# Pool bias of four token tiles added by accumulating transfers in a PoolFormer and ConvFFN layer

## The chip, the cores and the metric

The kernel runs on one core of one Trainium2 chip. The metric is the device time of one execution in microseconds. The core has five engines with a queue of instructions each: TensorE (PE, whose weight loads are listed as PEld), VectorE (DVE), ScalarE (ACT), GpSimd (POOL) and SyncE (SP). An engine works its instructions in their order; semaphores let one wait for another. Transfers (DMA) are issued by SP, ACT or POOL and move on 16 DMA engines. A transfer that adds its source to its destination (an accumulating transfer) is issued by POOL here.

## What is computed

One layer (DEPTH is 1) for 1024 tokens of 1024 channels, float32: a causal pooling mixer, then a gated FFN with a causal convolution of width 3.

```python
h = rms_norm(x, norm_mix_g)
# pooling, per group of 256 channels, windows 2, 4, 8, 16:
groups.append(window_sum / count - h_group)
y = pool_scale * (einsum('bsgc,gcd->bsgd', d, pool_w) + pool_b)
x = x + y
h = causal_depthwise_conv(rms_norm(x, norm_ffn_g) @ ffn_w_in, conv_w, conv_b)
val, gate = split(h, 2)
x = x + (silu(gate) * val) @ ffn_w_out
```

The bias that matters here is one row of 1024 numbers, pool_scale * pool_b, that is added to every token.

## The kernel before

**Mixer stage (the first 75 us of the span).** The tokens are eight tiles of 128. For tile j, in this order: `stat` (L442 on) takes the mean square on ACT (`junk_a`, L178) and refines the root on DVE (L180 to L183); `mixer_norm` scales the band matrices by it (`bandr`, L187); `window_sums` multiplies x by them on PE (`psd`, L201), which gives the pooled tile transposed; DVE adds the first 16 tokens' part from the tile before (L270); ACT copies it to SBUF (`dh`, L271); `mixer_out` multiplies by the scaled weights on PE (`psy`, L286), and two more matmuls with a matrix of ones add the bias, which lies in two rows, a high and a low part, so that the sum is exact enough (L289, `bias_hl`); DVE adds x (L292, "the residual add"), in place, which gives x1; SP writes x1 to DRAM. Then the statistics of x1 (`junk_b`, `st_b`), the normed tile `n` (L304), its transposes on PE (`pst`, L319), and the copies and splits that make the FFN's operands from them: ACT copies to `n2f` (L328, L331), ACT and DVE write a high part and a rest (`B`, `T`; L338, L339). The second four tiles are combined with the first four (L350), so they complete `T1`.

All of `psd`, `psy` and `pst` come from one pool of three PSUM tiles, taken in turn (`bank2`): a group of matmuls waits until the tile of three groups before has been read.

**FFN, one level of Strassen's scheme.** A weight tile (`win`, 1 MB, 22 of them) has four parts A11, A12, A21, A22, each 128x512. Products are formed from A11, A12, A22 and from the sums S1 = A21+A22, S2 = A11+S1, S3 = A11+A21, S4 = A12+S2. S3 and S1 of all weight tiles, and S2 and S4 of the first two, are made by accumulating transfers of 256 KB that POOL issues (L361), each waiting for the one it builds on and for the splits that still read its destination; the other sums are made by DVE. Each operand is then split in two (`split`, L91 on ACT, L92 on DVE). For weight tiles 0 and 1, `sums_in(n, 0)` makes S3 and S1, `sums_in(n, 1)` S2 and S4. S2 overwrites A11, so it waits for the A11 split; S4 overwrites A12 and waits for the A12 split.

**Order of the work.** The mixer's last loop, `for j in range(2, NS + 4)`, weaves tile j's steps together: windows of tile j-1, output of tile j-2, transposes of tile j-4. `prep_event(k)` puts a split of a weight tile between them: k = 0 and 1 are A11 of weight tiles 0 and 1, k = 2 and 3 their A12. `tc.issue_after(marks[...])` holds instructions behind a given one in the planned order; the tile framework's scheduler then puts the instructions of each engine in a fixed order.

Of the kernel before, what the change touches and what calls it, by code (L numbers as in the profile page):

```python
# [7 lines left out]
F32 = mybir.dt.float32  # L8
# [3 lines left out]
ALU = mybir.AluOpType  # L12
PSUM = bass.MemoryType.PSUM

P = 128
S = 1024
D = 1024
# [22 lines left out]
NOPS_A = 3  # L40

XBUFS = 5

PAD = 24

# [18 lines left out]
def trunk_kernel(ctx: ExitStack, tc: tile.TileContext, x, consts, par, rows, pool_w, w_in, w_out, out):  # L64
    nc = tc.nc

    const = ctx.enter_context(tc.tile_pool(name="const", bufs=1))
    dram = ctx.enter_context(tc.tile_pool(name="dram", bufs=1, space=bass.MemoryType.DRAM))
# [4 lines left out]
    work = ctx.enter_context(tc.tile_pool(name="work", bufs=1, side="right"))  # L73
# [24 lines left out]
    xs = {}  # L98
# [36 lines left out]
    for g, w in enumerate(WINDOWS):  # L135

        m = band[:, g, :]
# [30 lines left out]
    def rstd_of(src, name, halves=False):  # L168
        junk = pp.tile([P, D], BF16, tag="junk", name=f"junk_{name}")
        st = pp.tile([P, 8], F32, tag="st", name=f"st_{name}", bufs=8)  # L170
        part, first, ms, root, q, inv, half = (st[:, i : i + 1] for i in range(7))
        bias = eps_t
        if halves:
            bias = first
            nc.scalar.activation(junk[:, :NH], src[:, :NH], AF.Square, accum_out=half)
            nc.vector.tensor_scalar(first, half, D * EPS, None, op0=ALU.add)
            src, junk = src[:, NH:], junk[:, NH:]
        nc.scalar.activation(junk, src, AF.Square, accum_out=part)  # L178
        marks[name] = nc.scalar.activation(root, part, AF.Sqrt, bias=bias).ins
        nc.vector.tensor_scalar(ms, part, first if halves else D * EPS, None, op0=ALU.add)  # L180

        nc.vector.scalar_tensor_tensor(q, root, root, ms, op0=ALU.mult, op1=ALU.add)
        nc.vector.reciprocal(inv, q)  # L183
        return root, inv

# [30 lines left out]
    wps = pp.tile([P, 2 * NG, GRP], F32, tag="wps", name="wps")  # L216
# [13 lines left out]


    b8 = rows8[:, 1, :]

    def pool_bias():
        marks["bias"] = nc.scalar.activation(bias8[:, 0, :], b8, AF.Copy).ins
        marks["bias_dve"] = nc.vector.tensor_tensor(bias8[:, 1, :], b8, bias8[:, 0, :].bitcast(F32), ALU.subtract).ins
        for l in range(2):
            m = nc.sync.dma_start(bias_hl[l : l + 1, :].bitcast(F32), bias8[:, l, :].bitcast(F32)).ins
        with tc.issue_after(m):
            for j in range(3, NS):  # L240
                load_x(j)
            nc.sync.dma_start(par_sb[:, :GM], par[:, :GM])
# [14 lines left out]
    def window_sums(j):  # L257
        ps = bank2(f"psd{j}")
        marks[f"psd{j}"] = windows(ps, xs[j], bands.pop(j))
        return ps  # L260

    def mixer_window(j, ps=None):
        ps = window_sums(j) if ps is None else ps
        dh = ds[j] = pp.tile([P, NK, P], F32, tag="dh", name=f"dh{j}", bufs=2)
        ps3 = ps.rearrange("p (c s) -> p c s", c=NK)
        first = ps3[:, :, :HALO]
        if j == 0:
            marks["first"] = nc.vector.tensor_tensor(first, first, fac, ALU.mult).ins
        elif j > 1:
            nc.vector.tensor_tensor(first, first, edges[:, :, j * HALO : (j + 1) * HALO], ALU.add)  # L270
        marks[f"dh{j}"] = nc.scalar.activation(dh, ps3, AF.Copy).ins  # L271
# [9 lines left out]
    def mixer_out(j, stats=True):  # L281
        dh = ds.pop(j)
        ps = bank2(f"psy{j}")
        for c in range(NK):
            o = ps[:, c // 2 * GRP : (c // 2 + 1) * GRP]
            nc.tensor.matmul(o, dh[:, c, :], wps[:, c, :], start=c % 4 == 0, stop=False, skip_group_check=True)  # L286
        for h in range(2):
            cols = slice(h * NH, (h + 1) * NH)
            m = nc.tensor.matmul(ps[:, cols], ones, bias_hl[:, cols], start=False, stop=True, skip_group_check=True)  # L289
        marks[f"psy{j}"] = m.ins  # L290
        x1 = n2s[j] = xs.pop(j)
        marks[j] = nc.vector.tensor_tensor(x1, ps, x1, ALU.add).ins  # L292
        nc.sync.dma_start(x1_dram[j * P : (j + 1) * P, :], x1)
        if stats:
            mixer_out_stats(j)
# [62 lines left out]
    def sums_in(n, step):  # L358

        def more(out, a):  # L360
            nc.gpsimd.dma_start(out, a, accum_op=ALU.add)  # L361

        a11, a12, a21, a22 = (raws[n][:, i, k * NH : (k + 1) * NH] for i in range(2) for k in range(2))
        if step == 0:
            s3 = sums[n, "S3"] = tmp(f"S3_{n}")
            nc.sync.dma_start(s3, w_in[order[n]][:, 0, :NH])
            more(s3, a21)
            more(a21, a22)
        else:
            sums[n, "S2"] = a11  # L370
            more(a11, a21)
            sums[n, "S4"] = a12
            more(a12, a11)
# [95 lines left out]
    def prep_event(k):  # L469
        if k < len(events):  # L470
            n, p = events[k]
            prep_in(n, STEPS[p][0])
# [49 lines left out]
        mixer_edges()  # L522
    with tc.issue_after(marks["edges_pe"]):
        sums3 = window_sums(3)
    with tc.issue_after(marks["dh1+"]), tc.issue_after(marks["edges"]):
        mixer_out_stats(0)
    for j in range(2, NS + 4):
        if 3 < j < NS:
            with tc.issue_after(marks[1]) if j == 4 else nullcontext():
                mixer_norm(j)  # L530
        if 1 <= j - 1 < NS and j > 2:
            mixer_window(j - 1, {3: sums2, 4: sums3}.get(j))
        if j == NS + 1:
            with tc.issue_after(marks[f"n{NS - 2}"]):
                prep_event(4)
                prep_event(6)
        if 1 <= j - 2 < NS:
            with tc.issue_after(marks["S4", 0] if j == NS + 1 else marks[f"band{min(j, 4)}"]) if j > 2 else nullcontext(), tc.issue_after(marks["psd3"]):
                mixer_out(j - 2)
        if 0 <= j - 2 < NS:  # L540
            with tc.issue_after(marks["dh1+"]):
                ffn_norm(j - 2)
        if 0 <= j - 4 < NS:
            ffn_operand(j - 4)
        if j in (4, 6):
            load_in(j // 2 - 2)
            sums_in(j // 2 - 2, 0)
        if 5 <= j <= 8:
            with tc.issue_after(marks[j - 2]), tc.issue_after(marks[f"b{j - 3}"]):
                prep_event(j - 5)  # L550
        if j in (7, 8):
            sums_in(j - 7, 1)
        if j in (8, 10, 11):
            event((8, 10, 11).index(j))
        with tc.issue_after(marks["edges"]):
            stat(j + 1)
            stat(j + 2)
# [156 lines left out]
    for k in range(-SLOOK, len(oevents)):  # L714
        p, f = oevents[k + SLOOK] if k + SLOOK < len(oevents) else (None, 0)
# [8 lines left out]
        with tc.issue_after(lasts[-1]) if lasts else nullcontext():  # L724
# [12 lines left out]
            p, f = oevents[k]  # L737
# [10 lines left out]
        if f == 0 and opens:  # L748
            for i in range(4):
                tag = ("XXYY" if set_ == "X" else "YZZZ")[i]  # L750
# [106 lines left out]
```

## Time and profile before

| what | value |
|---|---|
| time, median of 3 runs | 672.28 us (670.89 to 673.64) |
| profiled execution, its time | 670.79 us |
| profiled execution, its span | 669.0 us |
| PE, DVE, ACT, POOL busy | 663.6, 569.1, 338.8, 47.8 us |
| granted PE clock | 1.00 |
| mixer stage, tile 0's windows to the first product with T1 | 7.6 to 74.9 us |

The profile is of one execution. A row of the timeline has the start in us from the start of the span, the length, the engine, the line of the kernel, the operation, what it writes and reads, and how many were merged; in brackets stands the idle time of the engine before it and what ended that. The buffers' numbers are left out there, so that `x` is any token tile and `win` any weight tile. Of a merged group of matmuls the length reaches from the start of the first to the end of the last, and consecutive groups overlap by the depth of the pipeline; from start to start is what a group costs. A row of the chain of waits has start, length, engine and line only. A DMA queue's row has its packets, MB, and the time of its packets as a share of 16 engines over the window asked for (q0 is the queue of the transfers that POOL issues, q1 that of SP). An issue row gives the KB of each and the median time from issue to landing.

### The profile page before, as it was taken

Reading aid. Unit: us, or ns where it says so; the run is one execution under the profiler, and the core shown is the slowest. Engines: PE = TensorE matmul, PEld = TensorE weight load, DVE = VectorE, ACT = ScalarE, POOL = GpSimd, SP = SyncE. Lnnn points to the kernel's source line nnn. Section 1 sums busy time; section 2 is a strip of 40 time slices with the busy share of each in tenths; the row PEclk is TensorE's granted clock in tenths of the full one; section 3 lists DMA queues with packets and bytes.
Section 4 is the critical chain, followed back from the end, with each engine's and each line's share of the span. In section 5 each row is a group of like instructions: output and inputs, shape, how many; then the busy total and the mean of one; then the engine's idle time right before and its main releaser. Section 6 shows DMA issues by size and latency. Waiting matters only on the chain.

```text
span 669.0 us, 8720 instructions
## 1 busy us (share of the span) xinstructions
PE 663.6 (99%) x3164; PEld 579.2 (87%) x3164; DVE 569.1 (85%) x841; ACT 338.8 (51%) x517; POOL 47.8 (7%) x73
## 2 busy tenths in 40 slices
PE   9999999999999999999999999999999999999997
PEld 7999878888888888888888888888888888888886
DVE  4798999998888888888888888887987988999995
ACT  6696656554544544444544454454554444444441
POOL 3021020111001111111011101100000000000000
PEclk9999999999999999999999999999999999999999
DMA  8983253544444454544444444429999710232231
GB/s 269 326 207 105 85 141 126 167 145 124 133 134 105 123 142 141 143 130 128 135 141 130 113 136 132 111 92 350 332 335 352 269 58 0 62 96 82 62 125 64
DMA packets 41603, 101.23 MB, mean 151 GB/s; under 512 B 4668, under 2 KB 6616, under 8 KB 38744
## 3 DMA queue, kind: packets, MB, share of 16 engines
q1 hardware_dynamic: 34464, 87.55, 37.3%
q0 software_dynamic: 6944, 12.59, 11.3%
q10 hardware_dynamic: 152, 0.53, 0.3%
q8 instruction: 25, 0.41, 0.2%
q14 instruction: 18, 0.15, 0.1%
HBM read 68.14 MB, written 19.92 MB: 132 GB/s over the span
## 4 chain that ended last, share of the span: by engine, by line
PE 96%; DVE 2%; ACT 1%; issue 0%; POOL 0%; ACTq 0%; POOLq 0%
PE oP L771 29%; PE Y L402 25%; PE X L402 17%; PE Z L402 16%; PE psy L286 4%; PE psd L201 2%; PE pst L319 1%; DVE T L339 1%; PE psy L289 1%; PE ps_scale L222 0%; PE idle_ps L149 0%; DVE n2f L580 0%; ACT B L338 0%; PE ps_edges L201 0%; PE ps_gain L248 0%
## 5 line engine op out<-in xcount | busy, mean ns | idle before, releaser
L771 PE MATMUL oP<-oBP,oAP 128*128 128x512 f32 (+1 forms) x924 | 198.9, 378 | 0.1
L771 PEld LDWEIGHTS oP<-oBP,oAP 128*128 128x128 f32 x924 | 174.0, 189 | 25.0 <-DVE oBP L92 0.5
L402 PE MATMUL X<-B,A11s 128*128 128x512 f32 x264 | 61.5, 380 | 0.0
L402 PE MATMUL Y<-T,S3s 128*128 128x512 f32 x264 | 60.8, 380 | 0.4 <-DVE q L431 0.4
L402 PE MATMUL Y<-T,A22s 128*128 128x512 f32 x264 | 60.8, 380 | 0.0
L402 PE MATMUL Z<-T,S1s 128*128 128x512 f32 x264 | 60.8, 379 | 0.0
L402 PE MATMUL X<-B,A12s 128*128 128x512 f32 x264 | 60.6, 379 | 0.0
L402 PE MATMUL Y<-T,S2s 128*128 128x512 f32 x264 | 60.6, 379 | 0.0
L402 PE MATMUL Z<-B,S4s 128*128 128x512 f32 x264 | 60.5, 379 | 0.0
L402 PEld LDWEIGHTS Y<-T,S3s 128*128 128x128 f32 x264 | 49.7, 189 | 8.2 <-DVE q L431 1.2
L402 PEld LDWEIGHTS Y<-T,A22s 128*128 128x128 f32 x264 | 49.7, 189 | 7.9 <-DVE hb L439 0.6
L402 PEld LDWEIGHTS Z<-T,S1s 128*128 128x128 f32 x264 | 49.8, 189 | 7.5 <-DVE T L339 0.4
L402 PEld LDWEIGHTS Z<-B,S4s 128*128 128x128 f32 x264 | 49.8, 189 | 7.3 <-DVE r L436 0.3
L402 PEld LDWEIGHTS Y<-T,S2s 128*128 128x128 f32 x264 | 49.9, 189 | 7.1
L402 PEld LDWEIGHTS X<-B,A11s 128*128 128x128 f32 x264 | 49.7, 189 | 7.3 <-DVE A11s L92 0.4
L402 PEld LDWEIGHTS X<-B,A12s 128*128 128x128 f32 x264 | 49.8, 189 | 7.0
L91 ACT ACTIVATE oBP<-blk 128x512 fp32r<-128x512 f32 x53 | 33.1, 625 | 44.2 <-PE oP L771 30.6
L460 ACT ACTIVATE gate<-gate 128x1024 f32<-128x1024 f32 x22 | 23.2, 1057 | 49.3 <-DVE gate L451 49.3
L91 ACT ACTIVATE oAP<-blk 128x512 fp32r<-128x512 f32 x55 | 34.1, 620 | 19.3 <-DVE blk L350 16.8
L92 DVE TENSOR_TENSOR oBP<-blk,oBP 128x512 fp32r<-128x512 f32 x53 | 36.5, 688 | 8.6 <-ACT oBP L91 6.6
L92 DVE TENSOR_TENSOR oAP<-blk,oAP 128x512 fp32r<-128x512 f32 x55 | 37.7, 685 | 2.6 <-ACT oAP L91 2.6
L450 DVE SCALAR_TENSOR_TENSOR val<-ha,par_sb,val 128x1023 f32<-128x1023 f32 x22 | 28.2, 1283 | 13.2 <-ACT val L449 13.2
(131 smaller groups left out, 958.3 us busy)
## 6 DMA issues: line engine op xcount, KB each, us to landing
win<-in_w_in_dram SPq DMA_DIRECT2D x22, 1024.0 KB, 4.8
g_dram<-val SPq DMA_DIRECT2D x22, 512.0 KB, 2.6
blk<-g_dram SPq DMA_DIRECT2D x33, 256.0 KB, 5.2
blk<-in_w_out_dram SPq DMA_DIRECT2D x31, 256.0 KB, 5.7
win<-win POOLq DMA_DIRECT2D x26, 256.0 KB, 3.5
S<-in_w_in_dram SPq DMA_DIRECT2D x22, 256.0 KB, 3.5
S<-win POOLq DMA_DIRECT2D x22, 256.0 KB, 4.2
A12s<-g_dram SPq DMA_DIRECT2D x22, 256.0 KB, 5.2
```

What stands on the lines that cost most here:

```text
L91: nc.scalar.activation(t[:, 0, :], src, AF.Copy)
L92: m = nc.vector.tensor_tensor(t[:, 1, :], src, t[:, 0, :].bitcast(F32), ALU.subtract)
L201: m = nc.tensor.matmul(ps[:, c * P : (c + 1) * P], src[:, c * P : (c + 1) * P], weights[:, c // 2, :], start=True, stop=True)
L286: nc.tensor.matmul(o, dh[:, c, :], wps[:, c, :], start=c % 4 == 0, stop=False, skip_group_check=True)
L289: m = nc.tensor.matmul(ps[:, cols], ones, bias_hl[:, cols], start=False, stop=True, skip_group_check=True)
L319: nc.tensor.transpose(ps[:, c * P : (c + 1) * P], n2[:, c * P : (c + 1) * P], ident)
L339: return hi, nc.vector.tensor_tensor(l, src, h.bitcast(F32), ALU.subtract).ins
L402: nc.tensor.matmul(bank, a[:, i, ks], woven(b[:, l, k, :]), start=opens and m == 0, stop=m == 11, skip_group_check=not opens)
L450: nc.vector.scalar_tensor_tensor(t[:, 1:], src[:, : S - 1], w[1], t[:, 1:], op0=ALU.mult, op1=ALU.add)
L460: nc.scalar.activation(gate, gate, AF.Silu)
L771: nc.tensor.matmul(bank, a[:, u, i * P : (i + 1) * P], woven(b[:, v, :])[:, c.start // 2 : c.stop // 2, :], start=opens and first, stop=g ...
```

## The change

Three parts.

1. For token tiles 4 to 7 (`BY_DMA = 4`) the two bias matmuls (L289) are left out. In their place the scaled bias row goes from SBUF to DRAM once, comes back spread to 128 rows (`bias_b`, in the buffer that held the edge tokens), and is added to x by an accumulating transfer of 512 KB per tile (`bias_into`), which waits for the tile's windows, since these read x, and which the residual add waits for. All six transfers are issued by POOL.
2. The refinement of the root (L182) is a tensor_scalar with two scalars from SBUF in place of a scalar_tensor_tensor; the result is the same.
3. `prep_event(0)` is issued one loop step later, and `prep_event(2)` moves to the step of `prep_event(1)`; the sum S1 of weight tiles 0 and 1 is issued from a step of its own, behind the bias transfer of tile 4 or 5.

```diff
+BY_DMA = 4
-        nc.vector.scalar_tensor_tensor(q, root, root, ms, op0=ALU.mult, op1=ALU.add)
+        nc.vector.tensor_scalar(q, root, root, ms, op0=ALU.mult, op1=ALU.add)
...
+    bias_row = dram.tile([1, D], F32, tag="bias_row", name="bias_row")
+    biased = {}
+    def bias_spread():
+        biased["tile"] = work.tile([P, D], F32, tag="ha", name="bias_b", bufs=1)
+        nc.gpsimd.dma_start(biased["tile"], bias_row.to_broadcast([P, D]))
+    def bias_into(j):
+        if j >= BY_DMA:
+            biased[j] = nc.gpsimd.dma_start(xs[j], biased["tile"], accum_op=ALU.add).ins
     def pool_bias():
...
+        nc.gpsimd.dma_start(bias_row.rearrange("o (k p) -> (o k) p", p=P), b8)
...
-        for h in range(2):
+        for h in range(0 if j >= BY_DMA else 2):
             cols = slice(h * NH, (h + 1) * NH)
             m = nc.tensor.matmul(ps[:, cols], ones, bias_hl[:, cols], start=False, stop=True, skip_group_check=True)
...
+        if step == 0 and n > 1 or step == 2:
             more(a21, a22)
-        else:
+        if step == 1:
...
     with tc.issue_after(marks["edges_pe"]):
         sums3 = window_sums(3)
+        bias_spread()
...
             mixer_window(j - 1, {3: sums2, 4: sums3}.get(j))
+            bias_into(j - 1)
...
-        if 5 <= j <= 8:
+        if j in (5, 6):
+            with tc.issue_after(biased[j - 1]):
+                sums_in(j - 5, 2)
+        if 6 <= j <= 8:
             with tc.issue_after(marks[j - 2]), tc.issue_after(marks[f"b{j - 3}"]):
-                prep_event(j - 5)
+                for k in {6: (0,), 7: (1, 2), 8: (3,)}[j]:
+                    prep_event(k)
```

What stands where now. In these rows a tile's buffer has its number. Before, token tiles 3 to 7 are x_225, x_227, x_229, x_231 and x_233, and weight tiles 0 and 1 are win_425 and win_550.

POOL, its transfers of the mixer stage, before:

```order
L361 DMA S_0_427<-win_425 128x512
L361 DMA win_425<-win_425 128x512
L361 DMA S_1_552<-win_550 128x512
L361 DMA win_550<-win_550 128x512
L361 DMA win_425<-win_425 128x512
L361 DMA win_550<-win_550 128x512
L361 DMA win_425<-win_425 128x512
L361 DMA win_550<-win_550 128x512
```

And after the change, where token tiles 3 to 7 are x_227, x_229, x_231, x_233 and x_235, and weight tiles 0 and 1 are win_429 and win_551:

```order
L376 DMA S_0_431<-win_429 128x512
L244 DMA x_229<-bias_b 128x1024
L376 DMA win_429<-win_429 128x512
L376 DMA S_1_553<-win_551 128x512
L244 DMA x_231<-bias_b 128x1024
L376 DMA win_551<-win_551 128x512
L376 DMA win_429<-win_429 128x512
L244 DMA x_233<-bias_b 128x1024
L376 DMA win_551<-win_551 128x512
L244 DMA x_235<-bias_b 128x1024
L376 DMA win_429<-win_429 128x512
L376 DMA win_551<-win_551 128x512
```

The three rows of win_425 and of win_429 are S1, S2 and S4 of weight tile 0, in that order, and likewise for tile 1. The bias of tile 7 (x_235) now stands ahead of S4 of weight tile 0. The write of the bias row and its spread come before the first row shown.

DVE, from the residual add of tile 5 to the split of the A12 part of weight tile 0, before:

```order
L292 TENSOR_TENSOR x_229<-psy_573,x_229 128x1024
L92 TENSOR_TENSOR A12s_610<-win_425,A12s_610 128x512
L339 TENSOR_TENSOR B_154<-pst_596,B_154 128x8x64
L180 TENSOR_SCALAR st_b_587<-st_b_587 128x1
L270 TENSOR_TENSOR psd_615<-psd_615,edges 128x8x16
```

After:

```order
L307 TENSOR_TENSOR x_231<-psy_575,x_231 128x1024
L94 TENSOR_TENSOR A11s_610<-win_551,A11s_610 128x512
L354 TENSOR_TENSOR B_155<-pst_596,B_155 128x8x64
L94 TENSOR_TENSOR A12s_613<-win_429,A12s_613 128x512
L182 TENSOR_SCALAR st_b_587<-st_b_587 128x1
L283 TENSOR_TENSOR psd_618<-psd_618,edges 128x8x16
```

The A11 split of weight tile 1 has come behind tile 5's add, and the A12 split of weight tile 0 behind a B part.

ACT, from the copy of tile 4's windows to the copy of tile 5's, before:

```order
L271 ACTIVATE dh_449<-psd_440 128x1024
L91 ACTIVATE A11s_489<-win_425 128x512
L338 ACTIVATE B_154<-pst_475 128x8x64
L178 ACTIVATE junk_b_465,st_b_466<-x_225 128x1024
L179 ACTIVATE st_b_466<-st_b_466,eps_t 128x1
L338 ACTIVATE B_156<-pst_475 128x8x64
L178 ACTIVATE junk_a_492,st_a_493<-x_233 128x1024
L328 ACTIVATE n2f<-pst_475 128x8x2x64
L179 ACTIVATE st_a_493<-st_a_493,eps_t 128x1
L271 ACTIVATE dh_510<-psd_501 128x1024
```

After:

```order
L284 ACTIVATE dh_452<-psd_443 128x1024
L353 ACTIVATE B_155<-pst_479 128x8x64
L180 ACTIVATE junk_b_469,st_b_470<-x_227 128x1024
L353 ACTIVATE B_157<-pst_479 128x8x64
L181 ACTIVATE st_b_470<-st_b_470,eps_t 128x1
L180 ACTIVATE junk_a_494,st_a_495<-x_235 128x1024
L343 ACTIVATE n2f<-pst_479 128x8x2x64
L181 ACTIVATE st_a_495<-st_a_495,eps_t 128x1
L284 ACTIVATE dh_512<-psd_503 128x1024
L93 ACTIVATE A11s_557<-win_429 128x512
```

The split of the A11 part of weight tile 0 has gone from ahead of tile 5's copy to behind it. In both orders ACT later does the S1 and S4 splits of weight tile 0 right before the `n2f` copy of tile 4's transposes.

More of the change, by code (lines that the diff above doesn't have):

```diff
@@ L285, in mixer_out @@
             o = ps[:, c // 2 * GRP : (c // 2 + 1) * GRP]
-            nc.tensor.matmul(o, dh[:, c, :], wps[:, c, :], start=c % 4 == 0, stop=False, skip_group_check=True)
-        for h in range(2):
+            m = nc.tensor.matmul(
+                o, dh[:, c, :], wps[:, c, :], start=c % 4 == 0, stop=j >= BY_DMA and c % 4 == 3, skip_group_check=True
+            )
+        for h in range(0 if j >= BY_DMA else 2):
             cols = slice(h * NH, (h + 1) * NH)
```

## The prediction

> **What bounds the kernel now.** I read the page first: the busy line of TensorE, then what the end of the chain hangs on.
>
> ```profile
> span 669.0 us, 8720 instructions
> PE 663.6 (99%) x3164; PEld 579.2 (87%) x3164; DVE 569.1 (85%) x841; ACT 338.8 (51%) x517; POOL 47.8 (7%) x73
> ```
>
> TensorE works 99% of the span, so a matmul taken away should shorten it, unless its helpers can't go faster. All that the change touches lies in the first 75 us, so next come the busy times of that stretch (columns: window, its length, then PE, weight load, DVE, ACT, POOL busy, clock, DMA share, GB/s).
>
> ```profile
> 20.00:30.00 10.00, 10.00 (x57) 8.93 (x56) 5.80 (x17) 7.27 (x13) 0.00 (x0) 1.00 0.97 339
> 40.00:45.00 5.00, 5.00 (x30) 4.41 (x29) 4.67 (x13) 4.97 (x11) 1.74 (x2) 1.00 0.76 188
> 45.00:50.00 5.00, 5.00 (x31) 4.59 (x30) 4.59 (x10) 4.56 (x8) 0.85 (x1) 1.00 0.88 210
> ```
>
> From 40 to 50 us PE, DVE and ACT are all above 90%: three engines of nearly the same length. The timeline of PE shows the end of tile 4's second half, and tiles 5 to 7:
>
> ```profile
> 42.95 0.81 PE L289 MATMUL psy<-bias_hl,ones 128*128 128x512 f32 x2
> 43.60 1.03 PE L319 MATMUL pst<-cst,n 128*128 128x128 f32 x8
> 44.48 2.05 PE L201 MATMUL psd<-bandr,x 128*128 128x128 f32 x16
> 46.36 3.62 PE L286 MATMUL psy<-wps,dh 128*128 128x256 f32 x16
> 49.63 0.82 PE L289 MATMUL psy<-bias_hl,ones 128*128 128x512 f32 x2
> 52.94 3.62 PE L286 MATMUL psy<-wps,dh 128*128 128x256 f32 x16
> 56.86 1.04 PE L319 MATMUL pst<-cst,n 128*128 128x128 f32 x8
> 64.25 1.91 PE L319 MATMUL pst<-cst,n 128*128 128x128 f32 x16
> ```
>
> Each group starts where the last one ends. Then the chain of waits in order of time: up to 71 us it is PE, then it leaves PE.
>
> ```profile
> 71.58 1.08 PE pst L319 x8
> 72.68 0.61 ACT n2f L331
> 89.27 0.61 DVE q L431
> 89.93 2.21 PE Y L402 x9
> ```
>
> From tile 7's transposes (71.58) to the q2 of the first weight tile (89.27) the end hangs on ACT and DVE, and DVE enters that stretch with tile 7's residual add. So what the change is worth is read from when DVE can start that add, 64.44 in the timeline of DVE:
>
> ```profile
> 38.16 1.22 DVE L292 TENSOR_TENSOR x<-psy,x 128x1024 f32<-128x1024 f32 x1
> 39.29 0.68 DVE L92 TENSOR_TENSOR A11s<-win,A11s 128x512 fp32r<-128x512 f32 x1
> 44.56 1.22 DVE L292 TENSOR_TENSOR x<-psy,x 128x1024 f32<-128x1024 f32 x1
> 47.00 0.15 DVE L180 TENSOR_SCALAR st_b<-st_b 128x1 f32<-128x1 f32 x1
> 48.25 0.21 DVE L182 SCALAR_TENSOR_TENSOR st_b<-st_b 128x1 f32<-128x1 f32 x1
> 50.48 1.22 DVE L292 TENSOR_TENSOR x<-psy,x 128x1024 f32<-128x1024 f32 x1 [0.30 <-PE psy L289]
> 51.62 0.68 DVE L92 TENSOR_TENSOR A12s<-win,A12s 128x512 fp32r<-128x512 f32 x1
> 57.06 1.22 DVE L292 TENSOR_TENSOR x<-psy,x 128x1024 f32<-128x1024 f32 x1 [0.96 <-PE psy L289]
> 63.24 0.68 DVE L92 TENSOR_TENSOR S4s<-win,S4s 128x512 fp32r<-128x512 f32 x1
> 64.44 1.22 DVE L292 TENSOR_TENSOR x<-psy,x 128x1024 f32<-128x1024 f32 x1 [0.53 <-PE psy L289]
> ```
>
> The adds of tiles 5, 6 and 7 wait for PE by 0.30, 0.96 and 0.53 us: PE leads, but DVE is never far behind.
>
> **Removed.** One pair of bias matmuls takes 43.60 - 42.95 = 0.65 us; four pairs are 2.6 us of PE. Were nothing else in the way, the add of tile 7 would come 2.6 us sooner.
>
> **What of it gets through.** Two rows of ACT stand beside tile 4 (the timeline of ACT; the others are used below):
>
> ```profile
> 37.63 0.63 ACT L91 ACTIVATE A11s<-win 128x512 fp32r<-128x512 f32 x1
> 43.40 1.02 ACT L271 ACTIVATE dh<-psd 128x1024 f32<-128x1024 f32 x1
> 56.47 0.64 ACT L91 ACTIVATE S4s<-win 128x512 fp32r<-128x512 f32 x1
> 57.94 0.60 ACT L331 ACTIVATE n2f<-pst 128x512 f32<-128x512 f32 x1 [0.83 <-PE pst L319]
> ```
>
> Tile 6's windows (44.48) take the PSUM that the copy at 43.40 leaves at 44.42: 0.06 us apart. With tile 4's pair gone PE is there at 43.83 and must wait for the copy. The moved A11 split takes 0.6 us of DVE (39.29, up to its successor at 39.89) and its ACT part out of this stretch, and the shorter refinements give some 0.25; walking DVE and ACT through their new order I get the copy at 43.04, 0.36 sooner, and the windows at 44.1. So some 0.4 of tile 4's 0.65 gets through. The same walk puts tile 5's add at 49.45 (1.0 sooner), tile 6's at 55.4 (1.6 sooner) and the end of tile 7's second half at 62.0 (2.2 sooner). So much is to be had if nothing is added.
>
> **The refinement.** A 128x1 tensor_scalar with an immediate takes 0.15 (47.00), the operation replaced 0.21 (48.25); with two scalars read from SBUF it isn't in the trace. Between 0.15 and 0.21 I take 0.15, the row of the same operation: 0.06 each, 17 times, on the path only where DVE is behind; it is in the walk.
>
> **Added: six transfers on POOL.** The bias row to DRAM and its spread to 128 rows lie where POOL idles and nothing needs their result before 33 us; they add 0.5 MB to a stretch where DMA is 97% busy (20 to 30), 1.5 us at 339 GB/s, in front of loads that are used from 44 us on. Without that slack they would cost these 1.5 us. The four accumulates are another matter. POOL issues in order, its transfers were these (timeline of POOL, then two DMA pages, of 42 to 47.5 and of 52.6 to 57, and an issue row):
>
> ```profile
> 42.10 1.74 POOL L361 DMA_DIRECT2D win<-win  x2 [3.22 <-DMA S<-win]
> 46.67 0.85 POOL L361 DMA_DIRECT2D win<-win  x1 [2.84 <-DVE A11s L92]
> 52.60 0.86 POOL L361 DMA_DIRECT2D win<-win  x1 [5.07 <-DVE A12s L92]
> ```
> ```profile
> q0 software_dynamic: 288, 0.52, 56.4%
> ```
> ```profile
> q0 software_dynamic: 144, 0.26, 34.8%
> q1 hardware_dynamic: 137, 0.50, 28.1%
> ```
> ```profile
> win<-win POOLq DMA_DIRECT2D x1, 256.0 KB, 3.3
> ```
>
> One 256 KB accumulate keeps the 16 DMA engines busy for 0.348 x 4.4 = 1.5 us and lands 3.3 us after its issue; two, 0.52 MB, keep them for 0.564 x 5.5 = 3.1 us. A bias accumulate has 512 KB. Bounds of its time in the queue: 0, if it runs wholly beside the others; 1.24 us, at the rate of a plain 512 KB write (28.1% of 4.4); 3.1, as the same bytes of accumulates. I take 3.1, the only row of accumulates.
>
> For tiles 4 to 6 that is hidden. Each is issued when its windows end (33.1, about 39.7, about 46) and needed by its add 9 to 11 us later. Tile 7's own is needed at 62 and lands near 58. But it stands in POOL's order ahead of the accumulate that makes S4 of the first weight tile, the one at 52.60 now.
>
> **What is late next.** S4 of weight tile 0 waits for that tile's A12 split. In the new order A11 of tile 1, a B11 part and A12 of tile 0 all follow tile 5's add (49.45 + 1.15 + 3 x 0.6), so the split ends at 52.5, against 52.3 (51.62 + 0.68) now. POOL then issues S2 of weight tile 1 at 51.3 (it was out at 46.67), tile 7's bias at 52.2, S4 at 53.1. Transfers: S2 from 52.65 (1.35 after issue, so that 1.35 + 1.5 + 0.4 make the 3.3) to 54.2, bias to 57.3, S4 to 58.8, landed at 59.2. ACT, in order, reaches its S4 split at 55.5, and behind it stands the copy of tile 4's transposes (57.94 now). It waits 3.7 us there and comes to the copy at 59.2 + 0.57 = 59.8. From that copy DVE needs 5.9 us to be free for tile 7's add (57.94 to 63.24 + 0.60), all but full in between; the same rows in the new order give 5.85. So the add starts at 65.6 instead of 64.44: 1.1 us later, not 2.2 sooner. DVE and ACT are the chain from there, so that stays: **+1.1 us**.
>
> Against the profiled execution's 670.79 us (span 669.0, 1.8 around it) that is 671.9; the median shown is 672.28, with runs from 670.89 to 673.64, so 673.4. By the bounds: with no queue time the S4 sum lands at 53.1 + 3.3 = 56.4 and the add is at 62.8, -1.6 us; with 3.1 and tile 6's x1 write (plain, 1.24 us, due in the same stretch) in front as well, +2.3. So the forecast's own range is 670.7 to 674.6.
>
> **Rivals.**
> First: the bias accumulate is cheap, near the plain rate of 1.24 us. Then S4 lands at 57.4, the add is at 63.8, -0.6 us: 671.7. For it: rows of 4 KB may pay less per byte than the 2 KB rows of all accumulates here; against it, two accumulates cost twice one. [...]
>
> Second: the full gain. If the S4 split is not what ACT waits for (the walk is off by some 3 us there), tile 7's add comes 2.2 sooner: 670.1. For it: DVE's waits for PE; against it, the order on POOL.
>
> Third, slower: tile 4's bias arrives late. Its accumulate goes out at 33.1 behind the S3 sum, which took 4.7 us there (row below); 4.7 + 3.1 = 7.8, landing near 41, needed at 44.15 where tile 4's add now can start. From then each us late is a us lost, since tile 6's bias stands on POOL behind a sum that waits for an A11 split behind that very add. With 7 us more (the spread and the loads of 20 to 30 us in each other's way) it lands at 48: +4, 676.
>
> ```profile
> S<-win POOLq DMA_DIRECT2D x1, 256.0 KB, 4.7
> ```
>
> **How the numbers follow.** Forecast (gain eaten by the S4 wait) 0.55; cheap accumulate 0.25; full gain 0.08; late bias 0.12. A measurement of this kernel can tell about 0.5%, 3.4 us, from no change. The whole of the PE time removed is less than that, so faster by over 0.5% needs scatter on top: 0.03 from the full gain, 0.03 from the cheap case, 0.01 from the forecast, 0.07 together. Slower: 0.08 from the late bias, 0.03 from the upper end of the forecast: 0.11. Within 0.5%: 0.82. The range for 8 in 10 takes in the full gain with the scatter of the median below it, and half of the late bias above: 669.4 to 675.4.
>
> **What would show it.** Right: no L289 rows after tile 3; psy to pst without a gap; ACT idle for 2 to 4 us before the S4 split near 56, released by a transfer; four 512 KB issues on POOL landing 5 to 6 us after issue; PE idle before tile 6's and 7's transposes; tile 7's add near 65.6. Wrong: the S4 split without a wait and tile 7's add near 62, or an add of tile 4 to 6 released by a transfer.

## The result, and the profile after

The changed kernel takes 676.13 us (median of 6 runs, 675.26 to 678.00); the kernel before, on the same chip, 671.18 us (6 runs, 670.77 to 673.64). The ratio is 1.0070, 95% interval 1.0049 to 1.0091: **slower by 0.5 to 0.9%, some 5 us**. The forecast was 673.4, with a range of 669.4 to 675.4, and most of the chance on a difference too small to tell. The sign of the forecast's sum was right (+1.1 us), its size was not, and the time lies above the range.

The profiled execution took 675.26 us. The head of its page, against 669.0 and 663.6 us before:

```profile
span 673.6 us, 8724 instructions
PE 663.4 (98%) x3156; PEld 578.6 (86%) x3156; DVE 569.2 (85%) x841; ACT 338.9 (50%) x517; POOL 52.1 (8%) x79
```

The span grew by 4.6 us, with eight matmuls fewer. So PE waits somewhere. Its timeline from tile 6's windows on:

```profile
44.07 2.05 PE L203 MATMUL psd<-bandr,x 128*128 128x128 f32 x16
62.45 1.04 PE L334 MATMUL pst<-cst,n 128*128 128x128 f32 x8
68.03 1.94 PE L334 MATMUL pst<-cst,n 128*128 128x128 f32 x8 [4.54 <-DVE n L319]
76.13 1.07 PE L334 MATMUL pst<-cst,n 128*128 128x128 f32 x8
```

The bias matmuls are gone, tile 6's windows start at 44.07, and the second half of tile 7 ends at 62.45: up to here the change gives what it promised. Then PE waits 4.54 us for the normed tile 6 (`n`), and tile 7's transposes, at 71.58 before, come at 76.13. DVE tells whom `n` waits for:

```profile
49.62 1.23 DVE L307 TENSOR_TENSOR x<-psy,x 128x1024 f32<-128x1024 f32 x1
51.96 0.68 DVE L94 TENSOR_TENSOR A12s<-win,A12s 128x512 fp32r<-128x512 f32 x1
55.73 1.22 DVE L307 TENSOR_TENSOR x<-psy,x 128x1024 f32<-128x1024 f32 x1 [0.38 <-PE psy L299]
63.73 1.28 DVE L365 TENSOR_TENSOR n2f<-n2f,pst 128x512 f32<-128x512 f32 x2 [6.18 <-ACT n2f L346]
69.01 1.22 DVE L307 TENSOR_TENSOR x<-psy,x 128x1024 f32<-128x1024 f32 x1
```

The residual adds of tiles 5 and 6 are sooner than before (49.62 and 55.73, against 50.48 and 57.06), and none of the adds waits for a transfer. Then DVE has nothing to do for 6.18 us, until ACT's copy of tile 4's transposes. ACT:

```profile
62.59 0.63 ACT L93 ACTIVATE S4s<-win 128x512 fp32r<-128x512 f32 x1 [6.87 <-DMA win<-win]
63.12 0.58 ACT L346 ACTIVATE n2f<-pst 128x512 f32<-128x512 f32 x1
```

ACT waits 6.87 us for the S4 sum of weight tile 0, and the copy stands behind it. The chain of waits has the same piece; before, this stretch of the chain was PE's:

```profile
53.17 9.39 DMA win<-win
62.59 0.63 ACT S4s L93
...
94.50 4.15 PE Y L418 x18
```

The piece is 9.39 us of one 256 KB transfer, from its issue at 53.17 to its landing, where the one before landed in 3.3. What is behind it keeps its distance: tile 7's add went from 64.44 to 69.01, +4.57, and the first product with q2 (`Y`) from 89.93 to 94.50, +4.57. The whole loss is there. What stood ahead of it on POOL, from tile 6's bias on (timeline), and how long the transfers of 52.5 to 53.3 took (DMA page, KB and us from issue to landing):

```profile
47.60 1.54 POOL L244 DMA_DIRECT2D x<-bias_b  x1
51.79 0.85 POOL L376 DMA_DIRECT2D win<-win  x1 [2.64 <-DVE A11s L94]
52.54 0.99 POOL L244 DMA_DIRECT2D x<-bias_b  x1
53.17 1.24 POOL L376 DMA_DIRECT2D win<-win  x1
```
```profile
x<-bias_b POOLq DMA_DIRECT2D x1, 512.0 KB, 9.2
win<-win POOLq DMA_DIRECT2D x1, 256.0 KB, 9.4
```

The order is the predicted one: S2 of weight tile 1 at 51.79, tile 7's bias at 52.54, the S4 sum at 53.17. The queues tell what the prediction left out (DMA pages of two windows, 53.2 to 62.5 and the one microsecond from 54 to 55):

```profile
q0 software_dynamic: 527, 1.27, 75.6%
q1 hardware_dynamic: 282, 1.03, 29.4%
```
```profile
q1 hardware_dynamic: 85, 0.35, 94.6%
q0 software_dynamic: 6, 0.01, 4.6%
```

Together the two queues fill the DMA engines (75.6 + 29.4 = 105%). In these 9.3 us 1.27 MB of accumulates moved, while S2 of weight tile 1, the bias and the S4 sum have 1.05 MB (taking MB as the page does): half of the rest is tile 6's bias, which was still under way at the start (0.11 MB in rows of 4 KB), half the beginning of weight tile 1's S4 sum (0.11 MB). And 1.03 MB are two writes of x1 by SP, of tile 5 and of tile 6. While the first is served, POOL's queue moves hardly anything; before that the write had waited for tile 6's bias (last section).

### The profile page after: what moved, and what is told of

It is laid out like the page before. It is cut to its first block, busy times and chain, and to the rows that moved or that the text cites. A ratio compares the mean times of both kernels' runs of the same rounds, so it can differ in the third digit from the quotient of the medians.

```text
span 673.6 us, 8724 instructions
## 1 busy us (share of the span) xinstructions
PE 663.4 (98%) x3156; PEld 578.6 (86%) x3156; DVE 569.2 (85%) x841; ACT 338.9 (50%) x517; POOL 52.1 (8%) x79
## 4 chain that ended last, share of the span: by engine, by line
PE 91%; DMA 3%; DVE 3%; ACT 2%; issue 1%; SPq 0%; ACTq 0%; DVEq 0%
PE oP L793 29%; PE Y L418 25%; PE X L418 16%; PE Z L418 15%; PE psy L299 3%; DMA win<-win 1%; PE psd L203 1%; PE pst L334 1%; DMA x_edge<-in_x_dram 1%; DMA x<-in_x_dram 1%; DVE T L354 1%; ACT B L353 0%; DVE n2f L602 0%; ACT junk_a L180 0%; ACT junk_b L180 0%
## 5 line engine op out<-in xcount | busy, mean ns | idle before, releaser
L418 PE MATMUL X<-B,A12s 128*128 128x512 f32 x264 | 60.7, 379 | 0.0
L418 PE MATMUL Z<-B,S4s 128*128 128x512 f32 x264 | 60.5, 379 | 0.0
L93 ACT ACTIVATE oBP<-blk 128x512 fp32r<-128x512 f32 x53 | 33.1, 625 | 44.1 <-PE oP L793 30.6
L376 POOL DMA_DIRECT2D S<-win x22 | 19.2, 873 | 267.8 <-DMA win<-in_w_in_dram 256.9
```

The lines of the kernel that those rows point to most:

```text
L93: nc.scalar.activation(t[:, 0, :], src, AF.Copy)
L418: nc.tensor.matmul(bank, a[:, i, ks], woven(b[:, l, k, :]), start=opens and m == 0, stop=m == 11, skip_group_check=not opens)
```

## Experiments

The theory from these rows: **the loss is the lateness of the S4 sum of weight tile 0**, through the transfers ahead of it (tile 7's bias, tile 6's bias that is not through, the writes of x1). The rivals: the moved splits or the two-scalar refinement cost something themselves; the adds get their bias late; the accumulates harm something that the chain does not show. Tile 7's bias, in front of that sum by the code's order, is the first suspect.

**No bias by transfer.** All tiles get it from PE as before; the moved splits and sums and the two-scalar refinement stay.

```diff
-BY_DMA = 4
+BY_DMA = ()
...
-    bias_row = dram.tile([1, D], F32, tag="bias_row", name="bias_row")
...
-        if j >= BY_DMA:
+        if j in BY_DMA:
...
-        nc.gpsimd.dma_start(bias_row.rearrange("o (k p) -> (o k) p", p=P), b8)
...
-        bias_spread()
...
```

> All eight tiles have their bias by matmuls again, the bias transfers and the spread are gone; the moved A11 splits and the refinement with two scalars stay. Theory (the accumulates in POOL's queue make the S4 sum of weight tile 0 late): the S4 sum is issued near 53 and lands near 56.3, ACT waits under 1 us for it, tile 7's add within 0.7 of 64.4, the time within 1 us of the kernel before (671.2). Rival (the moved splits or the refinement are what costs): the time stays 2 us or more above the kernel before.

Measured: 670.94 us against 670.74, ratio 1.0002 (0.9992 to 1.0011). ACT and DVE, timelines:

```profile
58.47 0.64 ACT L93 ACTIVATE S4s<-win 128x512 fp32r<-128x512 f32 x1 [1.55 <-DMA win<-win]
64.88 1.22 DVE L305 TENSOR_TENSOR x<-psy,x 128x1024 f32<-128x1024 f32 x1
```

The loss is gone with the transfers, so parts 2 and 3 alone don't make it. They do move the S4 sum: the A12 split of weight tile 0 behind an A11 split puts it at 54.37 (52.60 before), and ACT waits 1.55 us for it, where under 1 was expected. Tile 7's add is 0.44 later than before, but that is not their cost: tile 2's add, ahead of all moved splits, is already 0.45 later (32.08 for 31.63). The stage starts that much apart from one execution to the next.

**Tile 7's bias behind the S4 sum, and tile 7's bias by PE.** Two ways to take the 512 KB from in front of the sum (where `BY_DMA` is a list of tiles, the tests `j >= BY_DMA` become `j in BY_DMA`).

```diff
...
-            bias_into(j - 1)
+            with tc.issue_after(marks["S4sum", 0]) if j == 8 else nullcontext():
+                bias_into(j - 1)
```
```diff
-BY_DMA = 4
+BY_DMA = (4, 5, 6)
...
```

> One place changed on POOL: the bias of tile 7 goes out behind the S4 sum of weight tile 0. Theory: the S4 sum lands some 2.6 to 3 us sooner (512 KB at 0.2 MB/us less ahead of it), near 59.5 instead of 62.6, tile 7's add near 66 instead of 69.0, the time 3 us below the changed kernel, about 673. Rival (the queue is not served in order, or the delay is DMA load as such): the S4 sum lands within 1 us of 62.6 and the time stays near 676.

> Tiles 4 to 6 by accumulates, tile 7's bias by matmuls. Theory: the S4 sum as in the run before it, near 59.5; the 0.65 us of PE that come back are hidden in front of tile 7's add, so the time is the same as there, about 673. Rival (PE work counts in full): 0.65 us above that run.

Measured: 672.56 us (ratio 1.0022, 1.0012 to 1.0033) and 672.00 (1.0020, 1.0010 to 1.0030). ACT in the one, then in the other:

```profile
58.95 0.63 ACT L93 ACTIVATE S4s<-win 128x512 fp32r<-128x512 f32 x1 [3.28 <-DMA win<-win]
```
```profile
58.66 0.63 ACT L93 ACTIVATE S4s<-win 128x512 fp32r<-128x512 f32 x1 [2.98 <-DMA win<-win]
```

The sum is issued at 53.12 and 53.13, as in the change, and its split starts 3.64 and 3.93 us sooner. Tile 7's add is at 65.36 and 65.08 instead of 69.01: sooner by 3.65 and 3.93, the same. So 3.7 to 3.9 of the 4.6 us hang on this one transfer's place. But the sum still takes 5.5 to 5.8 us to land, not 3.3, and both kernels are slower than before: something else is ahead of it.

**The writes of x1 later.** Two tries. In the first the writes of tiles 4 to 6 are placed behind the S1 split in the planned order; in the second behind tile 7's own write on SP.

```diff
...
+        if j == NS + 1:
+            with tc.issue_after(marks["S1", 0]):
+                for i in (4, 5, 6):
+                    nc.sync.dma_start(x1_dram[i * P : (i + 1) * P, :], marks["x1", i])
```
```diff
...
+            with tc.issue_after(marks["x1"]):
...
```

> The changed kernel with the x1 writes of tiles 4 to 6 (512 KB each, by SP) put off until the S1 split of weight tile 0. Theory (the writes take the DMA engines from the accumulates one for one): two writes, of tiles 5 and 6, lie between 53 and 62.6 and take 1.3 us each, so the S4 sum lands 2 to 3 us sooner, near 60, and the time is near 673.5. Rival (the accumulates alone fill their queue, the writes run beside them): the S4 sum within 0.7 us of 62.6, the time near 676.

> As late_x1, but the writes of tiles 4 to 6 now stand on SP behind tile 7's own, which waits for its add, so they can't start before 69 us. Theory (writes and accumulates share the DMA engines one for one; three writes of 1.3 us lie between 45 and 62): the S4 sum lands 2.6 to 3.9 us sooner than 62.6, tile 7's add near 66, the time near 673. Rival: the accumulates alone set it, the S4 sum within 0.7 us of 62.6, the time near 676.

The first is a miss: 675.58 us (ratio 1.0071, 1.0048 to 1.0095). SP has nothing else to do there, so a place in the planned order held nothing; it issued the three writes from 45.74 on, as in the change (timeline of SP):

```profile
45.74 11.77 SPq L583 DMA_DIRECT2D x_dram<-x  x3
```

In the second they go out from 68.8 on. It takes 674.07 us (3 runs, 1.0043, 1.0028 to 1.0057). ACT, and the transfers issued at 51.75, 52.55 and 53.18 (DMA pages of three short windows: S2 of weight tile 1, the bias of tile 7, the S4 sum):

```profile
60.75 0.63 ACT L93 ACTIVATE S4s<-win 128x512 fp32r<-128x512 f32 x1 [5.02 <-DMA win<-win]
```
```profile
win<-win POOLq DMA_DIRECT2D x1, 256.0 KB, 3.3
...
x<-bias_b POOLq DMA_DIRECT2D x1, 512.0 KB, 5.5
...
win<-win POOLq DMA_DIRECT2D x1, 256.0 KB, 7.5
```

The split of S4 starts 1.84 us sooner than in the change, tile 7's add too (67.17). That lies between theory (2.6 to 3.9 us) and rival (within 0.7). Here S2 of weight tile 1 lands in 3.3 us, as the S4 sum did before, where it took 5.8 in the change: tile 6's bias lands at 53.2 (55.1 in the change), and no write stands behind it, so the queue is free when S2's data start: its first packet comes at 53.2, 1.4 us after its issue at 51.75.

**Tile 7's bias alone by transfer.** Tiles 4 to 6 get theirs from PE; the rest as in the change.

```diff
-BY_DMA = 4
+BY_DMA = (7,)
...
```

> Only tile 7's bias by an accumulate, tiles 4 to 6 by matmuls; it still stands ahead of the S4 sum. Theory (S4 is late by tile 7's own 512 KB and by the three before it, which keep the queue full from 42 us on): without these three the S4 sum lands 2 us or more sooner, at 59 to 60.5, tile 7's add at 65.5 to 67, the time at 672 to 673.5. Rival (tile 7's place alone decides): it lands at 62 or later, the time at 675 or more.

Measured: 674.56 us (2 runs, 1.0050, 1.0033 to 1.0067). ACT waits 5.01 us, as in the run with late writes; the sum lands at 61.6 and tile 7's add is at 68.08, between theory (59 to 60.5) and rival (62). Here the writes stand where they did, but no bias of tile 6 is in the queue, and the S4 sum again takes 7.5 us. So the 1.9 us between 9.4 and 7.5 are neither of the two alone: with the writes or with tile 6's bias it is 7.5, with both 9.4. With both, tile 6's bias and then tile 5's write are served ahead of S2.

**Part 1 of the change alone.** All four biases by transfer, with splits, sums and refinement as before the change.

```diff
...
-        if step == 0 and n > 1 or step == 2:
...
-        if step == 1:
+        else:
...
-                for k in {6: (0,), 7: (1, 2), 8: (3,)}[j]:
-                    prep_event(k)
+                prep_event(j - 5)
```

> All four biases by accumulates, but the A11 and A12 splits, the S1 sums and the refinement as in the kernel before. On POOL the S4 sum now stands ahead of tile 7's bias. Theory (order on POOL and a full queue): S4 is issued near 52 and lands near 57.5, ACT waits 2 us, tile 7's add near 64, the time 670 to 671.5; tiles 5 and 6 may wait a little for their bias. Rival (the transfers as such cost): 674 or more.

Measured: 674.34 us (1.0054, 1.0041 to 1.0068). DVE's tile 5 add, then POOL's issue of that tile's bias:

```profile
53.16 1.23 DVE L307 TENSOR_TENSOR x<-psy,x 128x1024 f32<-128x1024 f32 x1 [2.82 <-PE psd L203]
```
```profile
46.45 1.19 POOL L244 DMA_DIRECT2D x<-bias_b  x1
```

Without part 3 tile 5's bias stands on POOL behind a sum that waits 6.5 us for S3 of weight tile 1 to land, goes out at 46.45 (40.28 in the change) and lands 6.6 us later, at 53.05. The row names PE, but the bias landed 0.1 us before the add's start. This is a late bias: the adds of tiles 5 and 6 are at 53.16 and 58.83 instead of 49.62 and 55.73. The S4 sum makes ACT wait only 2.23 us, since ACT itself is late by then. The expected 670 to 671.5 us was missed; the time is the rival's.

**Tiles 3 to 5 by transfer, without parts 2 and 3.** With no bias of tiles 6 and 7 ahead of it the S4 sum should be free.

```diff
-BY_DMA = 4
+BY_DMA = (3, 4, 5)
...
```

> Tiles 3, 4 and 5 by accumulates, 6 and 7 by matmuls, splits, S1 sums and refinement as before. Three pairs are off PE (1.95 us) and no bias is issued after 41 us, so the queue is empty when S4 is issued near 52: it lands at 56 and ACT does not wait. Theory: tile 7's add near 63, the time 1.0 to 1.8 us below the kernel before, 669 to 669.8. Rival (PE time is not what bounds this stretch): within 0.4 us of the kernel before.

Measured: 674.75 us (1.0054, 1.0042 to 1.0067). I had expected less than before. The adds of tiles 3, 4 and 5 (DVE):

```profile
38.87 1.22 DVE L307 TENSOR_TENSOR x<-psy,x 128x1024 f32<-128x1024 f32 x1 [1.50 <-DMA x<-bias_b]
47.68 1.22 DVE L307 TENSOR_TENSOR x<-psy,x 128x1024 f32<-128x1024 f32 x1 [2.12 <-DMA x<-bias_b]
56.02 1.23 DVE L307 TENSOR_TENSOR x<-psy,x 128x1024 f32<-128x1024 f32 x1 [3.17 <-DMA x<-bias_b]
```

Every bias is late, and each by more than the last. The next ones stand on POOL behind sums that are late themselves; tile 4's goes out at 42.03, behind S1 of weight tile 0 (timeline of POOL):

```profile
41.49 0.87 POOL L376 DMA_DIRECT2D win<-win  x1 [8.32 <-DVE B L354]
42.03 1.22 POOL L244 DMA_DIRECT2D x<-bias_b  x1
```

That sum waited 8.32 us for a part of B, which DVE makes behind the late add of tile 3; S3, which it reads, had itself landed only at 41.0 (issued at 32.30, 8.7 us), so it could have gone at most 0.5 us sooner. ACT's S4 split doesn't wait at all, and tile 7's add is at 68.91: nearly the change's loss by another way. So a bias by transfer costs time in two places, at its own add and at the sum behind it, and what guards the one can harm the other.

**The S4 sum ahead of the S2 sum of weight tile 1.** Now the theory is turned round: if the lateness of that one sum is the loss, a kernel that puts it forward should keep what PE gains. The A12 split of weight tile 0 goes ahead of the A11 split of weight tile 1, by which POOL issues the S4 sum ahead of the other S2; the refinement is the old one. Four kernels: bias by transfer for tiles 4 and 5; for 4 to 6; for 4 to 6 with late writes of x1 (as above); for 4 to 7 with late writes and tile 7's bias behind the S4 sum.

```diff
-BY_DMA = 4
+BY_DMA = (4, 5)
...
-        nc.vector.tensor_scalar(q, root, root, ms, op0=ALU.mult, op1=ALU.add)
+        nc.vector.scalar_tensor_tensor(q, root, root, ms, op0=ALU.mult, op1=ALU.add)
...
-                for k in {6: (0,), 7: (1, 2), 8: (3,)}[j]:
+                for k in {6: (0,), 7: (2, 1), 8: (3,)}[j]:
```

> Bias of tiles 4 and 5 by accumulating transfers, tiles 6 and 7 by TensorE as before; the A12 part of weight tile 0 is split ahead of the A11 part of weight tile 1, so that POOL issues the S4 sum of weight tile 0 right behind its S2 sum and ahead of the S2 sum of weight tile 1; the refinement's replaced instruction is the old one. Theory (the loss of the change is the S4 sum of weight tile 0 that lands 9.4 us after its issue behind other transfers): the sum is issued near 52, with no bias of tiles 6 and 7 about it, and lands at 55.5 to 57; ScalarE waits for it under 1.5 us, tile 7's residual add starts at 63 to 64 where after has 69.01 and before 64.44, and the kernel takes 0.5 to 1.4 us less than before (about 670). Rival (the accumulates of tiles 4 and 5 cost the path something of their own, wherever the S4 sum stands): the add is at 65 or later and the time is that of before or above it.

> As the run with the bias of tiles 4 and 5 by transfers and the S4 sum of weight tile 0 ahead of the S2 sum of weight tile 1, with tile 6's bias by a transfer too (issued ahead of that S4 sum). Theory: the sum is issued near 52 behind one accumulate of 512 KB and one write of x1, and lands at 57 to 58.5; tile 7's second half is freed of 0.65 us of TensorE more, its residual add starts at 63.4 to 64.5 and the time is 0 to 1 us below before. Rival: tile 6's accumulate and the x1 writes together push the landing to 60 or later, the add is at 66 or later and the time 1 us or more above before.

> As the run before it (bias of tiles 4 to 6 by transfers, the S4 sum of weight tile 0 ahead of the S2 sum of weight tile 1), with the writes of x1 of tiles 4 to 6 placed on SyncE behind the write of tile 7, so that none of them stands among the sums. Theory (each write of 512 KB in front of the sum costs it 0.9 to 1.3 us): the S4 sum lands about 1 us sooner than with the writes in place, at 56 to 57.5; tile 7's residual add starts at 63 to 63.9 and the time is 0.5 to 1.5 us below before. Rival (with the sum that early the add waits for TensorE's work, not for the transfer): the add and the time are within 0.3 us of the run with the writes in place.

> As the run with late writes of x1, with tile 7's bias by a transfer too, issued behind the S4 sum of weight tile 0: all that the change wanted from TensorE is taken, and nothing of 512 KB is issued between tile 6's bias and that sum. Theory: the S4 sum lands at 56 to 57.5 as with tiles 4 to 6 alone, tile 7's bias lands by 61, before its add, and the add is 0.3 to 0.65 us sooner than with tiles 4 to 6, at 62.4 to 63.6: 0.8 to 2 us below before. Rival (tile 7's bias then delays the S2 sum of weight tile 1 and what follows): the add waits for the bias or the sums of weight tile 1 for their splits, and the time is at or above before.

Measured, against 670.80 us (32 runs): 670.24 (ratio 0.9996, 0.9987 to 1.0005), 670.37 (0.9995, 0.9986 to 1.0004), 669.91 (0.9985, 0.9976 to 0.9994) and 669.51 (0.9979, 0.9970 to 0.9989). The first two can't be told from before; the last two are faster, by 0.06 to 0.24% and 0.11 to 0.30%. The last one on ACT, DVE, PE and POOL, timelines:

```profile
55.69 0.64 ACT L93 ACTIVATE S4s<-win 128x512 fp32r<-128x512 f32 x1
62.68 1.23 DVE L307 TENSOR_TENSOR x<-psy,x 128x1024 f32<-128x1024 f32 x1
62.48 1.91 PE L337 MATMUL pst<-cst,n 128*128 128x128 f32 x16
51.82 0.85 POOL L379 DMA_DIRECT2D win<-win  x1 [3.21 <-DVE A12s L94]
52.56 1.00 POOL L244 DMA_DIRECT2D x<-bias_b  x1
53.26 1.19 POOL L379 DMA_DIRECT2D win<-win  x1
```

The sum goes out at 51.82, lands in 3.3 us, and ACT does not wait. PE goes from tile 7's second half to the transposes without a gap, tile 7's add is at 62.68, 1.76 sooner than before, and the span is 667.2, 1.8 shorter. Now S2 of weight tile 1 is the one behind the bias, with 7.3 us to land, and nothing on the chain is waiting for it. The brackets for the add held in all four; the sum goes out at 52.8 to 53.4 in the first three, where I had thought 52, and lands sooner than I had thought in the last (55.1). The late writes bring the add forward by 0.55 us (63.74 for 64.29), but tile 2's add is already 0.21 sooner there (32.00 for 32.21): the 0.34 left is close to the 0.3 of their rival, which is not clearly refuted. What the old refinement alone is worth in these four was not tried.

All runs side by side, from the profiled execution of each (the profiled execution of before: 670.79 us, span 669.0):

| kernel | S4 sum issued | us to landing | ACT waits | tile 7's add | span |
|---|---|---|---|---|---|
| before | 52.60 | 3.3 | 0 | 64.44 | 669.0 |
| the change | 53.17 | 9.4 | 6.87 | 69.01 | 673.6 |
| no bias by transfer | 54.37 | 4.1 | 1.55 | 64.88 | 669.4 |
| tile 7's bias behind the sum | 53.12 | 5.8 | 3.28 | 65.36 | 669.9 |
| tile 7's bias by PE | 53.13 | 5.5 | 2.98 | 65.08 | 669.6 |
| writes later, first try | 53.37 | 8.8 | 6.27 | 68.61 | 674.2 |
| writes later, second try | 53.18 | 7.5 | 5.02 | 67.17 | 671.7 |
| tile 7's bias alone | 54.11 | 7.5 | 5.01 | 68.08 | 672.6 |
| part 1 alone | 55.28 | 6.2 | 2.23 | 67.86 | 672.3 |
| tiles 3 to 5, parts 2 and 3 off | 58.14 | 3.3 | 0 | 68.91 | 673.4 |
| S4 forward, tiles 4, 5 | 52.83 | 3.4 | 0.47 | 63.55 | 668.1 |
| S4 forward, tiles 4 to 6 | 53.42 | 4.5 | 1.31 | 64.29 | 668.8 |
| same, writes later | 53.31 | 3.8 | 0.73 | 63.74 | 668.3 |
| S4 forward, tiles 4 to 7, writes later | 51.82 | 3.3 | 0 | 62.68 | 667.2 |

The span less the start of tile 7's add is 604.4 to 604.6 us in every row but one: so what the change is worth is read from that add, over a range of 6 us. The one is the first try at the writes, with 605.6: there PE's granted clock is 0.50 until 73.5 us instead of 71.3 (last section), PE's X products (69.23 on) run right up to tile 7's transposes, and these come 8.20 us after the add (76.81) instead of 7.12.

Small differences between rows are not to be read as effects: tile 2's add, which comes ahead of the moved splits and needs no bias transfer, stands anywhere from 31.33 to 32.21 us in these executions. Counted from it, the four kernels with S4 forward bring tile 7's add 0.60, 0.73, 1.07 and 1.53 us closer than before.

## Why the prediction was wrong, point by point

- **What bounds the kernel, and where the change's worth is read.** Right, as the table shows.
- **Removed, and what gets through.** Right: tile 6's windows at 44.07 (44.1 predicted), tile 5's add at 49.62 (49.45), tile 6's at 55.73 (55.4), the end of tile 7's second half at 62.45 (62.0). With the S4 sum forward 1.76 us of the 2.2 reach tile 7's add (1.53 counted from tile 2's add).
- **The refinement.** Wrong in sign. The rows of the new form are above both ends I took (timeline of DVE, after):

```profile
47.05 0.27 DVE L184 TENSOR_SCALAR st_b<-st_b 128x1 f32<-128x1 f32 x1
```

  With two scalars from SBUF it takes 0.27 us, 0.06 more than the 0.21 it replaced, where I took 0.06 less: 0.12 on each of 17, few of them on the path. No run shows it alone; in the run without transfers of bias, counted from tile 2's add, parts 2 and 3 together move tile 7's add by nothing (32.80 us, 32.81 before).
- **Tile 4 to 6's accumulates are hidden.** Right, but with little to spare: 8.3, 8.5 and 7.5 us from issue to landing, where I expected 5 to 6; tile 6's landed at 55.1, its add started at 55.73. The third rival, the late bias, did not come in the change because part 3 puts the biases ahead of the S1 sums on POOL; with part 3 undone it came at once (tile 5's add, 53.16 for 49.62).
- **What is late next: the step that failed.** The place, the order on POOL, the engine that waits and what stands behind it (+5.9 us from the copy to the add: 63.12 to 69.01) all were as written. The size of one term was not, the transfers up to the landing of S4: "S2 from 52.65 to 54.2, bias to 57.3, S4 to 58.8, landed at 59.2". It landed at 62.56, 3.4 later, and the add came 3.4 later (69.01 for 65.6). Two things were left out. First, the transfers were laid end to end from an empty queue, and it wasn't empty: tile 6's bias landed only at 55.1, and tile 5's write was served behind it, ahead of S2. In the run with late writes, where neither is in S2's way, S2 and the sum land 2.5 and 1.9 sooner after their issue. Second, that run's sum still lands 1.5 later than the 59.2 (53.18 + 7.5 = 60.7). The packets in its trace tell where: a 256 KB sum has 144 packets, 16 of them of 4 bytes, which I take for the ends of the 16 DMA engines' shares; 15 of the sum's are through by 58.78, as I had it, the last one at 60.34, and the landing at 60.7 comes behind the last (62.22 and 62.56 in the change). At 58.39 the instruction queue (q8) moves 16 KB, 1.03 us on one engine. In the change the ends are 61.11 and 62.22, and the 16 KB come at 59.70 (DMA page, 59 to 60; 6.0% of 16 engines is 0.96 us of one):

```profile
q8 instruction: 1, 0.02, 6.0%
```

  With tile 7's bias alone by transfer they come at 59.37 (ends 59.77 and 61.26); before, at 55.83, when the S4 sum is done, and there all 16 end within 0.2 us. The trace doesn't say which engine moved the 16 KB, so that it is the late one is inferred from these coincidences.
- **The upper bound** had tile 6's write in it, as one plain write of 1.24 us added to the sum. Two writes ran: tile 5's ahead of S2 (94.6% of the engines from 54 to 55), tile 6's when the S4 sum was nearly through. Tile 6's bias ahead of them and the one late engine were in no term. So the bound of +2.3 was below the measured 4.6. A bound built by adding one neighbour to a chain that starts from an empty queue is not a bound.
- **The cheap accumulate.** Refuted. 512 KB in rows of 4 KB cost about what the same bytes in rows of 2 KB do (0.336 us a row against 0.187, mean of the packets from 30 to 64 us in the run with late writes: 10% less for each byte): from 53.2 to 62.5 POOL's queue moved 1.27 MB at 75.6% in the change (shown above), and 0.79 MB at 50.1% in the run without transfers of bias (below), where all its rows have 2 KB. That is 0.181 (rows of both kinds) and 0.170 MB for each us in which all 16 engines serve it.

```profile
q0 software_dynamic: 432, 0.79, 50.1%
```

  So the 3.1 us that I took for 512 KB was about right (0.52 MB by 0.181 is 2.9), and the runs that take tile 7's bias from ahead of the sum bear it out (3.6 to 3.9 us).
- **The full gain** was refuted in the change: its condition was that ACT does not wait for the S4 split. In the kernel that met it (S4 forward, tiles 4 to 7, writes later), most of the gain was there: 1.8 us of span and 1.3 of the median, for 2.2 in the rival's sum.
- **The chances.** Slower by over 0.5% had 0.11. Both the likeliest case and its upper end lay below that line because the one transfer's time was built from an empty queue and 16 even engines.

## What to carry to other kernels

Work that is moved from a full engine to a transfer costs what the transfer delays: ask who stands behind it in its queue, and who waits for that; here 512 KB landed in front of a 256 KB sum, which took 9.4 us to land instead of 3.3 and for which a copy, a normed tile and then PE waited. Take the time of such a transfer from what all queues hold when it is issued, the plain writes of another engine too, and not from its neighbours' durations laid end to end. And before such a change is given up, look at its order: the same four biases cost 0.7% in one order of sums and writes and saved 0.2% in another (with the old refinement).

## What was not expected of the hardware

**Plain writes and accumulates were served in blocks.** In the change 0.35 MB of x1 moved from 54 to 55 us and 0.01 MB of accumulates, though S2 of weight tile 1, the bias and the S4 sum were in the queue. But the write had no precedence: SP issued it at 50.87 (tile 5's), and from 52 to 53 the engines served POOL's queue alone, with tile 6's bias:

```profile
q0 software_dynamic: 51, 0.20, 104.8%
```

It likewise went with tile 6's write: issued at 56.99, it moved nothing from 58 to 60 us and 0.31 MB from 61 to 62, behind tile 7's bias and the S4 sum. So here a 512 KB write that SP issued counted as one more transfer in line; what sets the turns between the queues was not shown.

**PE's clock after a pause.** At the end of the 4.54 us without work (63.49 to 68.03) the granted clock fell to a half, 0.50 from 67.92 to 71.33 us, and the eight transposes took 1.94 us instead of 1.04 (columns: window, its length, busy us of PE, weight load, DVE, ACT, POOL, clock, DMA share, GB/s; the change):

```profile
66.00:68.00 2.00, 0.00 (x0) 0.00 (x0) 1.90 (x5) 0.93 (x2) 0.00 (x0) 0.98 0.00 0
68.00:70.00 2.00, 1.97 (x9) 2.00 (x10) 2.00 (x3) 0.00 (x0) 0.00 (x0) 0.50 0.00 0
```

In the change it cost the end nothing: from tile 7's add to tile 7's transposes it is 7.12 us here and 7.14 before, since DVE and ACT are the chain there. In the first try at the writes, where the half clock lasted twice as long (66.7 to 73.5 us), it cost 1.0 us. The length of the pause does not decide alone. With tile 7's bias alone by transfer PE paused 2.21 us and the clock fell all the same, to 0.50 from 67.32 to 70.73 us; in the second try at the writes it paused 2.69 us and the clock stayed at 1.00 (one window of each, first that of the run with tile 7's bias alone):

```profile
68.00:70.00 2.00, 2.00 (x9) 1.73 (x8) 2.00 (x4) 0.67 (x1) 0.00 (x0) 0.50 0.00 0
```
```profile
66.00:68.00 2.00, 1.81 (x13) 1.73 (x14) 2.00 (x4) 0.00 (x0) 0.00 (x0) 1.00 0.00 0
```

What decides whether the clock falls was not shown: the shorter of the two pauses lowered it, the longer one did not.
